# Layer 1's projections of the first sequence as seven block products

## The chip, the cores and the metric

The kernel runs on one core of a Trainium2 chip. The time is the device time of one execution in microseconds (us). TensorE is the matrix engine (PE in the rows; PEld is its weight loads), VectorE is DVE, ScalarE is ACT, GpSimd is POOL, and SP is the engine whose queue issues the DMAs. Each engine runs its own instructions in order and waits on semaphores for the others.

## The reference

Two sequences, p of 1024 tokens and s of 512, with 1024 channels, go through the same two layers. All is in float32.

```python
def trunk(x, ...):
    for layer in range(2):
        mix = even_mixer(x, ...) if layer % 2 == 0 else odd_mixer(x, ...)
        x = layer_norm(ALPHA * x + mix, ln_g[layer], ln_b[layer])

def odd_mixer(x, w_in, q_norm_g, k_norm_g, w_out):          # layer 1
    proj = x @ w_in                                          # [T,1024] @ [1024,2560]
    q, k, v, z = jnp.split(proj, IN1_SPLIT_POINTS, axis=-1)  # 1024, 256, 256, 1024
    q = rms_norm(q.reshape(B, T, 8, 128), q_norm_g)
    k = rms_norm(k.reshape(B, T, 2, 128), k_norm_g)
    q, k = apply_axial_rope(q, cos, sin), apply_axial_rope(k, cos, sin)
    o = blocked_attention(q, k, v)                           # 8 query heads, 2 of k and v
    return (o * jax.nn.silu(z)) @ w_out
```

`even_mixer` (layer 0) is a pooling mixer and a bidirectional mLSTM behind one input projection; the change leaves its work as it is.

## The kernel before, in words

Every matrix product is made of three: each float32 operand is split into a rounded high half and the rest, and `mm` is called for high by high, high by low and low by high. A weight unit is 128 channels by 512 columns (256 KB). `wunit` loads it through SP, GpSimd makes its high half (`hi_pool`), VectorE the low one (`lo_dve`). `mm` is line L97 for every product, so groups are told apart by the names of their tiles.

The stages follow one another:

1. Layer 0's first stage, to about 173 us: the projection of both sequences by weights `wt`. The x blocks (`xrp`, `xrs`) are loaded and split in its first piece.
2. The heads of layer 0, to about 600 us.
3. The mid stage, to about 759 us: layer 0's output projection (`o0p`, `o0s`) by tiles of 128 tokens, its layer norm, the store of the result to `x1` in DRAM, and, a tile or two later, eight transposes of the tile (`x1t`), whose split halves (`XH`, `XL`) stay in SBUF for layer 1. `mid_tiles` lists the tiles, p's eight and then s's four. The last head's transposes (`hTs`) lie among its first tiles.
4. kv of layer 1 (`layer1_kv`, 759 to 831 us): eight weight units, twelve tiles of 128 tokens. `tok_proj` gives a tile of 512 columns, k and v; v is split, k goes through `rope` and a transpose.
5. q (`layer1_qz`, 831 to 975 us): two pieces of 512 columns, each eight units, for twelve tiles. `rope` does the norm's sum of squares on ACT, the power on GpSimd (L929), the products with the tables on VectorE (L931, L936) and their sum on GpSimd (L937); four transposes (`Tq`), an ACT copy and a store to DRAM follow.
6. z (`z_block`, 975 to 1104 us): eight blocks of 128 columns by 1024 channels for three groups of 512 tokens, with silu on ACT and a store. The first unit's scores (`Sp`) are woven into the last blocks.
7. Attention and the output projection, to the end.

The order of the instructions of an engine is the order in which the program's scheduler puts them by its own model of costs, from the order of the code. It is fixed when the program is built. Tiles are taken from rings with a set number of buffers (`bufs`), and PSUM banks too (`mm` 2, `me` 3, `mx` 1, `mc` 2): an instruction that writes one waits for the last reader of the tile before.

Of the kernel before, what the change touches and what calls it, by code (L numbers as in the profile page):

```python
# [56 lines left out]
class Kern:  # L57
    def __init__(self, ctx, tc, a):
# [5 lines left out]
        self.z0, self.xcd = {}, {}  # L64
        self.wlight = False
# [188 lines left out]
    def layer0(self, seqs):  # L254
# [4 lines left out]
        with ExitStack() as ctx:  # L259
# [4 lines left out]
            with ExitStack() as c1:  # L264
# [6 lines left out]
                self.wbufs, self.rbufs = 10, 4  # L271
                self.gate_places(gp)
# [620 lines left out]
    def mid_spread(self, t, y):  # L893

        _, _, gi, i = self.mid_tiles[t]
        c = slice(i * P, (i + 1) * P)
        for half in range(2):
            pt = self.bank("mc", f"x1t{gi}{i}{half}")
            for j in range(4):
                k = 4 * half + j  # L900
                self.nc.tensor.transpose(pt[:, j * P:(j + 1) * P], y[:, k * P:(k + 1) * P], self.idn)
            for j in range(2):
                xh, xl = (x[gi][2 * half + j][:, :, c] for x in (self.XH, self.XL))
                pv = pt[:, 256 * j:256 * j + 256].rearrange("p (k t) -> p k t", t=P)
                self.hi_act(xh, pv)
                self.lo_dve(xl, pv, xh)
# [12 lines left out]
    def rope(self, ps, nh, n, tabs, t1, t2, name):
# [11 lines left out]
        nc.vector.tensor_tensor(out=t1[:, 0:W].rearrange("p (h f) -> p h f", f=P), in0=ps.rearrange("p (h f) -> p h f", f=P),  # L931
# [8 lines left out]
    def rope_consts(self, which, g, tiles):  # L940
        nc = self.nc
        self.load(g.rearrange("p a f -> p (a f)"), self.a["g4"][256 * which:256 * which + 256].partition_broadcast(P))
        for i, n in enumerate(("cos", "sin")):
            t = tiles[i]
            self.load(t, self.a[n])
            nc.vector.tensor_tensor(out=t, in0=t, in1=g[:, i:i + 1, :].to_broadcast([P, 8, P]), op=ALU.mult)
# [13 lines left out]
    def layer1_kv(self):  # L960

        nc, a, hp = self.nc, self.a, self.hp
        tags = iter([f"x{p}{k}{h}" for h in (1, 0) for k in range(KD) for p in "lh"])
        place = lambda name, shape=(P, 512): self.x0p.tile(list(shape), F32R, tag=next(tags), name=name)
        self.Kh, self.Kl, self.Vh, self.Vl, self.rq = {}, {}, {}, {}, {}
        for s in self.seqs:
            T = self.seqs[s][0]
            self.Kh[s], self.Kl[s] = ([[place(f"K{x}{s}{kv}{c}") for c in range(T // 512)] for kv in range(2)] for x in "hl")
            self.Vh[s], self.Vl[s] = ([place(f"V{x}{s}{c}", (P, 2, 256)) for c in range(T // 256)] for x in "hl")
            self.rq[s] = self.cp.tile([P, T // P, 8], F32, name=f"rq{s}")  # L970
        self.spare = list(tags)
# [12 lines left out]
        g = self.raw("rg1", (P, 2, P))
        tabs = self.rope_consts(1, g, [hp.tile([P, 8, P], F32, tag=("w", "pl")[i], name=f"rt1{i}") for i in range(2)])
        for gi, (s, g) in enumerate(self.groups):
            for i in range(4):
# [360 lines left out]
```

## Time and profile before

| | us |
|---|---|
| median of three runs | 1557.92 |
| the three runs | 1551.84, 1557.92, 1557.95 |
| profiled execution | 1552.2 |
| its span | 1550.5 |
| TensorE's mean granted clock | 0.979 of full speed |

Three kinds of views are used below. The windows give, for a stretch of time, each engine's busy time with its count of instructions, TensorE's granted clock, the DMA engines' share and GB/s. The chain of work that ended last is followed back from the last instruction, each step to what released it. Rows of instructions give the start, the length, the line and the operation (out<-in); matmuls overlap, so their pace is read from one start to the next. A group's row has the busy time and the mean length in ns.

### The profile page before, as it was taken

What the parts mean: (1) busy time and instruction counts of PE and PEld (TensorE: products, weight loads), DVE (VectorE), ACT (ScalarE), POOL (GpSimd) and SP (SyncE); (2) the same over time, 40 slices, a digit from 0 to 9 for tenths busy, and PEclk for the clock granted to TensorE, in tenths of its full rate; (3) what the DMA queues carried; (4) which work ended last, traced back from release to release, by engine and by line L of the source; (5) the groups of instructions that cost most, each with busy time, mean ns of one, the idle gap of its engine ahead of it and who ended that gap; (6) DMA issues with size and microseconds to landing.
All of it is one profiled execution on the core that took longest, in us unless ns stands there. A gap on an engine that the chain in (4) does not pass through costs nothing.

```text
span 1550.5 us, 20820 instructions
## 1 busy us (share of the span) xinstructions
PE 1489.5 (96%) x7166; PEld 1221.7 (79%) x7166; DVE 921.7 (59%) x1894; ACT 666.3 (43%) x1522; POOL 630.8 (41%) x652
## 2 busy tenths in 40 slices
PE   8999998999997899999999999999989999999997
PEld 7877787878876778777778888888778888888886
DVE  5242265586867888847754452311377777777775
ACT  4122354455545665334221332213565555555651
POOL 3101234343464654535433454301244444454642
PEclk9999999999998899999999999999999999999999
DMA  7302342234434556444502131321241111111211
GB/s 229 122 30 69 95 123 95 96 103 129 144 122 150 179 168 198 150 141 152 172 7 88 59 102 55 122 89 69 66 138 28 55 55 55 55 55 55 82 62 55
DMA packets 125305, 155.77 MB, mean 100 GB/s; under 512 B 9472, under 2 KB 71424, under 8 KB 125200
## 3 DMA queue, kind: packets, MB, share of 16 engines
q1 hardware_dynamic: 125200, 154.45, 31.3%
q8 instruction: 56, 0.92, 0.2%
q14 instruction: 49, 0.40, 0.1%
HBM read 107.18 MB, written 47.24 MB: 100 GB/s over the span
## 4 chain that ended last, share of the span: by engine, by line
PE 62%; DVE 15%; DMA 10%; issue 5%; ACT 4%; POOL 3%; SPq 0%; DVEq 0%; ACTq 0%; POOLq 0%
PE q L97 9%; PE z L97 8%; PE Sp L97 6%; PE Op L97 6%; PE o1p L97 5%; PE ptp L1134 4%; PE kv L97 3%; PE o1s L97 3%; PE tp L97 3%; PE zp L97 2%; PE ts L97 2%; PE zs L97 2%; PE Ss L97 1%; PE Os L97 1%; DMA wo0r<-wo 1%
## 5 line engine op out<-in xcount | busy, mean ns | idle before, releaser
L1112 POOL TENSOR_SCALAR prp<-prp,smp 128x1024 f32<-128x1024 f32 x64 | 72.7, 1136 | 137.6 <-DVE smp L1111 131.3
L87 ACT CAST pwp<-ptp 128x512 fp32r<-128x512 f32 x128 | 74.8, 584 | 95.0 <-PE ptp L1134 94.7
L97 PE MATMUL Op<-pwp,Vhp 128*128 128x512 f32 x256 | 109.0, 426 | 1.4 <-DVE pwp L90 1.4
L90 DVE TENSOR_TENSOR pwp<-ptp,pwp 128x512 fp32r<-128x512 f32 x128 | 87.3, 682 | 29.1 <-ACT pwp L87 29.1
L1107 ACT ACTIVATE prp<-Sp,nbp,rqp 128x1024 f32<-128x1024 f32 (+1 forms) x68 | 78.7, 1158 | 27.1 <-DVE nbp L1104 20.7
L1099 DVE TENSOR_REDUCE nbp<-Sp 128x1 f32<-128x1024 f32 (+1 forms) x68 | 78.2, 1153 | 15.7 <-PE Sp L97 15.6
L1134 PEld LDWEIGHTS ptp<-idn,prp 128*128 128x128 f32 x512 | 63.7, 140 | 21.5 <-POOL prp L1112 2.2
L1134 PE MATMUL ptp<-idn,prp 128*128 128x128 f32 x512 | 77.1, 272 | 3.4 <-POOL prp L1112 1.8
L97 PE MATMUL z<-x1h,wz_h 128*128 128x512 f32 x192 | 76.0, 396 | 0.0
L97 PE MATMUL z<-x1l,wz_h 128*128 128x512 f32 x192 | 75.7, 394 | 0.0
L97 PE MATMUL z<-x1h,wz_l 128*128 128x512 f32 x192 | 75.6, 395 | 0.0
L97 PE MATMUL q<-wq_h,x1l 128*128 128x512 f32 x144 | 57.2, 398 | 0.0
L97 PE MATMUL q<-wq_l,x1h 128*128 128x512 f32 x144 | 56.8, 396 | 0.0
L97 PE MATMUL q<-wq_h,x1h 128*128 128x512 f32 x144 | 56.3, 400 | 0.0
L97 PEld LDWEIGHTS Op<-pwp,Vhp 128*128 128x128 f32 x256 | 48.3, 189 | 8.8 <-DVE pwp L90 1.9
L97 PE MATMUL tp<-wt_h,xhp 128*128 128x512 f32 x128 | 51.1, 409 | 2.8 <-ACT wqk_r L248 2.8
L97 PE MATMUL o0p<-wo0h,ah0p 128*128 128x512 f32 x128 | 50.5, 400 | 1.9 <-DVE xr0p L835 1.9
L97 PE MATMUL o0p<-wo0l,ah0p 128*128 128x512 f32 x128 | 50.6, 396 | 0.7 <-POOL wo0l L94 0.7
L97 PE MATMUL tp<-wt_h,xlp 128*128 128x512 f32 x128 | 51.0, 404 | 0.0
L97 PE MATMUL tp<-wt_l,xhp 128*128 128x512 f32 x128 | 50.9, 402 | 0.0
L97 PE MATMUL o0p<-wo0h,al0p 128*128 128x512 f32 x128 | 50.7, 397 | 0.0
L97 PE MATMUL Op<-pwp,Vlp 128*128 128x512 f32 x128 | 50.1, 391 | 0.0
(804 smaller groups left out, 4691.9 us busy)
## 6 DMA issues: line engine op xcount, KB each, us to landing
wt_r<-w0t SPq DMA_DIRECT2D x16, 256.0 KB, 4.5
xrp<-xT_p SPq DMA_DIRECT2D x16, 256.0 KB, 3.6
xrs<-xT_s SPq DMA_DIRECT2D x16, 256.0 KB, 3.2
wp<-rd_p SPq DMA_DIRECT2D x16, 256.0 KB, 5.0
z_p<-zsp SPq DMA_DIRECT2D x16, 256.0 KB, 3.4
szp<-z_p SPq DMA_DIRECT2D x16, 256.0 KB, 3.0
wo0r<-wo SPq DMA_DIRECT2D x16, 256.0 KB, 4.4
ar0p<-act_p SPq DMA_DIRECT2D x16, 256.0 KB, 2.9
```

The source lines that it names most:

```text
L87: self.nc.scalar.copy(out, in_)
L90: self.nc.vector.tensor_tensor(out=out, in0=in_, in1=hi.bitcast(F32), op=ALU.subtract)
L97: self.nc.tensor.matmul(out, lhsT=lhsT, rhs=rhs, start=start, stop=stop)
L1099: nc.vector.tensor_reduce(out=nb[:, i:i + 1], in_=b, op=ALU.max, axis=AX.X, negate=True)
L1107: nc.scalar.activation(pr[:, i * W:(i + 1) * W], b, AF.Exp, bias=nb[:, 0:1], scale=rq, accum_out=sm[:, i:i + 1])
L1112: nc.gpsimd.tensor_scalar(pr, pr, sm, 0.0, ALU.mult, ALU.add)
L1134: nc.tensor.transpose(pt[:, h * P:(h + 1) * P], prs[h][:, c * P:(c + 1) * P], self.idn)
```

## The change

For p alone, kv, z and q of layer 1 are taken by the scheme of Strassen and Winograd. The tokens are two halves and the channels two halves, so x is four blocks A11, A12, A21, A22; the weight of a q piece pair, of a z block pair or of kv (k and v columns) is four blocks as well. In place of eight block products there are seven, P1 to P7, four of them with a sum of x blocks or a sum of weight blocks on a side, or both. Their results are added into the four output blocks.

```diff
+    PRODUCTS = (("P1", "A11", (0, 0)), ("P2", "A12", (1, 0)), ("P6", "S2", 1), ("P5", "S1", 0),
+                ("P3", "S4", (1, 1)), ("P7", "S3", 2), ("P4", "A22", 3))
```

A number in the last place is a sum of weights, a pair is a plain block.

- `weight_sums`, in layer 0's first stage: ten sets (kv 2, q 4, z 4). A set is four loads of 256 KB, four subtractions (two on GpSimd, two on VectorE) and four stores to DRAM. Two sets are begun behind each of five groups of that stage.

```diff
+                for o, e, x, y, d in ((0, nc.gpsimd, (0, 1), (0, 0), (0, 0)), (2, nc.vector, (1, 1), (0, 1), (0, 1)),
+                                      (1, nc.gpsimd, (1, 1), (0, 0), (1, 1)), (3, nc.vector, (1, 1), (1, 0), (1, 0))):
+                    e.tensor_tensor(out=r[d], in0=r[x], in1=r[y], op=ALU.subtract)
+                    self.load(self.sums[kind][k, o], r[d])
...
+                        if piece or gi:
+                            for _ in range(2):
+                                next(presums, None)
```

- `mid_pair`, in the mid stage: tiles of p are taken in pairs, one of each half, and the list of tiles is reordered to 0, 4, 1, 5, 2, 6, 3, 7. Behind the transposes come the halves of A11, A12, A22 and, by adds on VectorE, of S1, S2 and S3 (high half on ACT, low half on GpSimd). S4 = A12 - S2 is made in kv, behind P2 (`last_sum`), on VectorE and GpSimd by turns.

```diff
+    K.mid_tiles = [("p", 4 * g + i, g, i) for i in range(4) for g in range(2)] + [("s", i, 2, i) for i in range(4)]
...
+        s1 = f("s1", ("y0", "sza")[i % 2])
+        nc.vector.tensor_tensor(out=s1, in0=a21, in1=p22, op=ALU.add)
...
+        nc.vector.tensor_tensor(out=s2, in0=s1, in1=p11, op=ALU.subtract)
+        nc.vector.scalar_tensor_tensor(out=a21, in0=a21, scalar=-1.0, in1=p11, op0=ALU.mult, op1=ALU.add)
```

- The products. kv's have 256 columns and are done first, then z (`z_pair`, four pairs of blocks), then q. For each product and tile `gathered` adds the result on VectorE (P1 is an ACT copy) to the running sums `u` and, where an output block is complete, to a tile `c`; P7 needs two such adds.

```diff
+                for k in range(4):
+                    ah, al = self.a_part(b, k)
+                    wh, wl = (w[:, k % nk * W:(k % nk + 1) * W] for w in cur[k // nk])
+                    self.mm(ps, ah[:, c], wh, k == 0, False)
+                    self.mm(ps, ah[:, c], wl, False, False)
+                    self.mm(ps, al[:, c], wh, False, k == 3)
+                self.gathered(prod, i, ps, u, W, finish, f"{name}{i}")
...
+        if prod in done:
+            o, a = done[prod]
+            c = a if prod in ("P7", "P4") else self.tp.tile([P, 512], F32, tag="c", name=f"c{name}{o}", bufs=2)[:, 0:W]
+            add(c, a, ALU.subtract if prod == "P4" else ALU.add)
+        if prod == "P1":
+            nc.scalar.copy(u2, ps)
+        elif prod in ("P6", "P7"):
+            add(u2, u2)
+        elif prod == "P5":
+            add(u4, u2)
+        if prod in done:
+            finish(o, i, c)
```

- For p the high halves of weights are made on ACT (`prepare`), and rope's first product on GpSimd instead of VectorE (`mul`).

```diff
-        nc.vector.tensor_tensor(out=t1[:, 0:W].rearrange("p (h f) -> p h f", f=P), in0=ps.rearrange("p (h f) -> p h f", f=P),
+        mul.tensor_tensor(out=t1[:, 0:W].rearrange("p (h f) -> p h f", f=P), in0=ps.rearrange("p (h f) -> p h f", f=P),
                                 in1=ct[:, n:n + 1, :].to_broadcast([P, nh, P]), op=ALU.mult)
```

- s comes behind p: its x1 is read back from DRAM and transposed there, and kv, q and z are done for it as before, with the weights loaded and split a second time. The first scores are woven into z's blocks of s.

```diff
+            y = self.x1p.tile([P, D], F32, tag=f"x1{'hl'[i % 2]}0{i // 2}", name=f"y1{i}")
+            self.load(y, self.x1[s][i])
...
+        units = [self.wunit(a["w1kv"][k], f"wkv{k}") for k in range(KD)]
```

In counts: matmuls of 512 columns for p go from 384 to 336 in q and in z; in kv 192 of 512 columns become 336 of 256. Weight units loaded for p go from 40, shared with s, to 70, and s loads 40 of its own.

Three places show how the instructions now stand.

First VectorE in kv of p. Before, in the middle of kv (`Vlp` and `Klp` are low halves of v and k, `kr` a k row, `ssk` its sum of squares, L931 and L936 rope's products, L999 the scaling):

```order
L90 TENSOR_TENSOR Vlp1_7510<-kv03_7719,Vhp1_7506 128x256
L90 TENSOR_TENSOR Klp10_7503<-kT01_7663,Khp10_7499 128x128
L999 TENSOR_SCALAR kr02_7699<-kr02_7699,rsk02_7704 128x128 x2
L927 TENSOR_SCALAR ssk03_7747<-ssk03_7747 128x2
L931 TENSOR_TENSOR kr03_7746<-kv03_7719,rt10_7571 128x256
L936 TENSOR_TENSOR kr03_7746<-kv03_7719,rt11_7572 128x128 x2
L999 TENSOR_SCALAR kr03_7746<-kr03_7746,rsk03_7751 128x128 x2
L90 TENSOR_TENSOR Vlp2_7511<-kv10_7766,Vhp2_7507 128x256
L90 TENSOR_TENSOR Klp00_7501<-kT02_7710,Khp00_7497 128x128
```

After, where P6 and P5 end (`u` the running sums, `ckv` a finished block, L975 to L977 and `S4l` the sum S4, `wlkv` the low half of a weight unit, `rt` rope's tables, L1006 rope's second product):

```order
L977 TENSOR_TENSOR s4a0_7953<-s4a0_7953,s4b0_7954 128x512
L1016 TENSOR_TENSOR rt1kp_7731<-rt1kp_7731,rgkp_7729 128x1024
L1094 TENSOR_TENSOR u11_7726<-u01_7722,kvP5i1_8075 128x256
L91 TENSOR_TENSOR wlkv06_7794<-kv011_r_7795,whkv06_7793 128x512
L91 TENSOR_TENSOR S4l0_7949<-s4a0_7953,S4h0_7945 128x512
L1006 TENSOR_TENSOR kr110_7820<-ckv011_7818,rt1kp_7731 128x128 x2
L1006 TENSOR_TENSOR kr111_7855<-ckv111_7853,rt1kp_7731 128x128 x2
L91 TENSOR_TENSOR wlkv17_7800<-kv111_r_7801,whkv17_7799 128x512
L975 TENSOR_TENSOR s4a2_7967<-A12h1_6724,A12l1_6726 128x512
L1094 TENSOR_TENSOR ckv211_7888<-u02_7723,kvP2i2_7875 128x256
L1094 TENSOR_TENSOR ckv311_7923<-u03_7724,kvP2i3_7910 128x256
L976 TENSOR_TENSOR s4b2_7968<-S2h1_6728,S2l1_6730 128x512
```

The k rows of one tile, which stood together, are parted by S4's sums, the tables, weight units and the adds that free TensorE's banks.

Second GpSimd at the end of q of p. Before, in the middle of q (`tq` is a q row, `wq1` a weight unit of the second piece):

```order
L937 TENSOR_TENSOR tq021_8672<-tq021_8672 128x512
L84 TENSOR_SCALAR wq14_h_8820<-wq14_r_8818 128x512
L84 TENSOR_SCALAR wq15_h_8826<-wq15_r_8824 128x512
L84 TENSOR_SCALAR wq16_h_8832<-wq16_r_8830 128x512
L84 TENSOR_SCALAR wq17_h_8838<-wq17_r_8836 128x512
L929 TENSOR_TENSOR rsq022_8728<-ssq022_8722,mhalf_83 128x4
L937 TENSOR_TENSOR tq022_8721<-tq022_8721 128x512
L929 TENSOR_TENSOR rsq023_8777<-ssq023_8771,mhalf_83 128x4
L937 TENSOR_TENSOR tq023_8770<-tq023_8770 128x512
```

After, at P4, where p ends and s begins (`t0qp` is a q row of p, L1001 rope's first product, L999 the power, L1007 the sum, `wkv` the kv weight units of s):

```order
L85 TENSOR_SCALAR wkv1_h_10096<-wkv1_r_10094 128x512
L85 TENSOR_SCALAR wkv2_h_10102<-wkv2_r_10100 128x512
L999 TENSOR_TENSOR rsqp123_9625<-ssqp123_9619,mhalf_86 128x4
L1007 TENSOR_TENSOR t0qp123_9617<-t0qp123_9617,t1qp123_9618 128x512
L85 TENSOR_SCALAR wkv3_h_10108<-wkv3_r_10106 128x512
L999 TENSOR_TENSOR rsqp220_9688<-ssqp220_9682,mhalf_86 128x4
L1001 TENSOR_TENSOR t0qp220_9680<-u10_7725,rt0qp_8426 128x512
L999 TENSOR_TENSOR rsqp221_9727<-ssqp221_9721,mhalf_86 128x4
L1007 TENSOR_TENSOR t0qp220_9680<-t0qp220_9680,t1qp220_9681 128x512
L1001 TENSOR_TENSOR t0qp221_9719<-u11_7726,rt0qp_8426 128x512
L85 TENSOR_SCALAR wkv4_h_10114<-wkv4_r_10112 128x512
L85 TENSOR_SCALAR wkv5_h_10120<-wkv5_r_10118 128x512
```

A row has three operations in place of two, and the units that s's kv tiles need stand among p's last four rows.

Third SP in layer 0's first stage, around the last x block of the first group. Before:

```order
L81 DMA wqT_r_355<-wqT 128x512
L81 DMA wkT_r_361<-wkT 128x512
L81 DMA xrp70_307<-xT_p 128x512
L81 DMA xrp01_397<-xT_p 128x512
L81 DMA xrp11_415<-xT_p 128x512
L81 DMA xrp21_433<-xT_p 128x512
L81 DMA xrp31_451<-xT_p 128x512
```

After (`srkv` are the loads for the sums, `sum_kv` the stores of them):

```order
L82 DMA xrp01_400<-xT_p 128x512
L82 DMA srkv010_560<-w1kv 128x2x256
L82 DMA srkv100_570<-w1kv 128x2x256
L82 DMA srkv101_572<-w1kv 128x2x256
L82 DMA srkv111_574<-w1kv 128x2x256
L82 DMA xrp11_418<-xT_p 128x512
L82 DMA srkv110_576<-w1kv 128x2x256
L82 DMA xrp21_436<-xT_p 128x512
L82 DMA sum_kv_57<-srkv000_554 128x512
L82 DMA sum_kv_57<-srkv001_556 128x512
L82 DMA xrp31_454<-xT_p 128x512
L82 DMA sum_kv_57<-srkv011_558 128x512
```

The x blocks `xrp01` to `xrp31` of p's second group, which stood next to each other, have loads for the sums between them, and `xrp31` stands behind two stores that wait for the subtractions.

More of the change, by code (lines that the diff above doesn't have):

```diff
@@ L64, in __init__ @@
         self.z0, self.xcd = {}, {}
+        self.sums = {n: d.tile([k, 4, P, 512], F32, name=f"sum_{n}") for n, k in (("kv", 2), ("q", 4), ("z", 4))}
         self.wlight = False
@@ L891, in mid_tile, with turned @@
         self.pend.append((t, xr))
-    def mid_spread(self, t, y):
-        _, _, gi, i = self.mid_tiles[t]
-        c = slice(i * P, (i + 1) * P)
[L897 to L906, printed above, removed]
+    def turned(self, y, half, tag, name):
+        pt = self.bank(tag, name)
+        for j in range(4):
+            k = 4 * half + j
+            self.nc.tensor.transpose(pt[:, j * P:(j + 1) * P], y[:, k * P:(k + 1) * P], self.idn)
+        return pt
@@ L921, in rope, with a_part @@
+    def a_part(self, b, k):
+        if b == "S4":
+            return tuple(x[k] for x in self.S4)
+        return tuple(x[k // 2][:, k % 2, :] for x in self.A[b])
+    def rope(self, ps, nh, n, tabs, t1, t2, name, mul):
         nc = self.nc
@@ new lines, in next_units, with gathered @@
+    def next_units(self, n):
+        while len(self.ready) < self.wbufs:
+            u = next(self.coming, None)
+            if u is None:
+                break
+            self.prepare(u, *(self.wp.tile([P, 512], F32R, tag=t, name=f"{t}{u[0]}{u[1]}{len(self.ready)}", bufs=self.wbufs) for t in ("wh", "wl")))
+        out, self.ready = self.ready[:n], self.ready[n:]
+        return out
+    def gathered(self, prod, i, ps, u, W, finish, name):
+        nc = self.nc
+        u2, u4 = (x[i][:, 0:W] for x in u)
+        add = lambda out, a, op=ALU.add: nc.vector.tensor_tensor(out=out, in0=a, in1=ps, op=op)
+        done = {"P2": ("11", u2), "P3": ("12", u4), "P7": ("22", u4), "P4": ("21", u2)}
+        if prod in done:
[10 more added lines that the diff above has]
+            finish(o, i, c)
@@ new lines, in token_products @@
+    def token_products(self, name, nk, W, u, finish, after=None):
+        for j, (prod, b, _) in enumerate(self.PRODUCTS):
+            cur = self.next_units(4 // nk)
+            for i in range(4):
+                ps = self.bank(("mm", "me")[i % 2], f"{name}{prod}i{i}")[:, 0:W]
+                c = slice(i * P, (i + 1) * P)
+                for k in range(4):
+                    ah, al = self.a_part(b, k)
[4 more added lines that the diff above has]
+                self.gathered(prod, i, ps, u, W, finish, f"{name}{i}")
+            if after and j == 1:
+                after()
@@ new lines, in layer1_in, with kv_done @@
+        table = lambda which, names, nt=8: self.rope_consts(which, tp.tile([P, 2, P], F32, tag="rg", name=f"rg{names}"),
+                                                            [tp.tile([P, nt, P], F32, tag=f"rt{i}", name=f"rt{i}{names}") for i in range(2)], nt)
+        tabs = table(1, "kp")
+        group = {"1": 0, "2": 1}
+        def kv_done(o, i, c):
+            g = group[o[0]]
+            if o[1] == "1":
+                self.k_rows(p, g, i, c, tabs, tp.tile([P, 2, 256], F32, tag="t", name=f"kr{o}{i}", bufs=4), self.nc.gpsimd)
+            else:
+                self.v_rows(p, 4 * g + i, c)
@@ L1238, in layer1 @@
                         weights(1, range(KD))
[L1239 removed]
+                        ts = [tp.tile([P, 512], F32, tag="c", name=f"ln1{j}", bufs=2) for j in range(2)]
                         ts += [self.raw(f"ln1{j}") for j in range(2, 4)]
```

297 lines of the change are left out of this document (198 added, 99 removed).

## The prediction

> **What bounds the kernel now.** I read the page's busy times first, then a table of the projection stage and its neighbours by windows, the chain of work that ended last inside that stage, TensorE's waits just before it, and single rows for prices.
>
> Busy times of the page, then the windows (us, us of each engine with its count, granted clock, DMA share, GB/s):
>
> ```profile
> PE 1489.5 (96%) x7166; PEld 1221.7 (79%) x7166; DVE 921.7 (59%) x1894; ACT 666.3 (43%) x1522; POOL 630.8 (41%) x652
> ...
> 0.00:173.00 173.00, 165.80 (x716) 131.86 (x717) 61.70 (x85) 46.26 (x76) 28.96 (x51) 0.96 0.32 107
> ...
> 600.00:759.00 159.00, 149.89 (x711) 122.76 (x710) 115.37 (x283) 62.44 (x135) 80.37 (x71) 0.99 0.52 166
> 759.00:831.00 72.00, 71.47 (x326) 57.60 (x326) 39.27 (x123) 18.67 (x84) 22.43 (x31) 1.00 0.11 35
> 831.00:975.00 144.00, 144.00 (x669) 117.26 (x669) 64.54 (x189) 40.76 (x218) 70.01 (x65) 1.00 0.28 84
> 975.00:1104.00 129.00, 129.00 (x560) 104.11 (x558) 22.95 (x45) 33.47 (x57) 18.96 (x24) 1.00 0.28 92
> ```
>
> TensorE is busy 96% of the span. Layer 1's kv (759 to 831), q (to 975) and z (to 1104) leave it idle for half a microsecond in 345 us at full clock, and the next busiest engine reaches 55% of a stage (VectorE in kv). So the chain there is matmul after matmul (start, length, count):
>
> ```profile
> 804.56 5.57 PE kv L97 x24
> ...
> 984.48 58.80 PE z L97 x253
> ```
>
> 58.80/253 = 0.2324 us for each matmul of 512 columns. What is taken off here is time, unless something new makes TensorE wait.
>
> **The products.** A product over one block of p (512 tokens by 512 channels in, 512 columns out) is four tiles of 12 matmuls. q and z: eight block products each became seven: 2 x 384 matmuls become 2 x 336, 96 fewer: 96 x 0.2324 = 22.3 us. kv: 192 matmuls of 512 columns become 336 of 256. The trace has none of 256, but neighbours:
>
> ```profile
> 297.06 0.27 PE L97 MATMUL Ap<-vhp,plp 128*128 128x130 f32 x1
> 297.17 0.34 PE L97 MATMUL Up<-vwhp,ktp 128*128 128x260 f32 x1
> ...
> 297.47 0.40 PE L97 MATMUL Up<-vwhp,ktp 128*128 128x260 f32 x2
> 297.71 0.28 PE L97 MATMUL Up<-vwlp,ktp 128*128 128x260 f32 x1
> 297.83 0.28 PE L97 MATMUL Up<-vwhp,ktp 128*128 128x260 f32 x1
> 297.95 0.39 PE L97 MATMUL xbp<-xhp,xbp2u_h 128*128 128x512 f32 x1
> ```
>
> 260 columns start 0.12 us apart (130 columns 0.11), each with a weight load of its own. 336 x 0.12 = 40.3 against 192 x 0.2324 = 44.6: 4.3 less. Together **-26.6 us**. The transposes are as many as before.
>
> A weight load lasts longer than that pace:
>
> ```profile
> L97 PEld LDWEIGHTS z<-x1h,wz_h 128*128 128x128 f32 x192 | 36.1, 188 | 8.3
> ```
>
> The Trainium skill, Perfetto Trace Analysis, section Identifying the Most-Contended Engine, tells one to judge TensorE by the summed time of weight loads rather than by matmul time. The rows above speak against adding these up: loads of 0.188 us passed at a pace of 0.12, so they overlap. By the page's measure the halved columns of kv would gain nothing; that is a rival below.
>
> **kv: VectorE becomes as full as TensorE.** Prices:
>
> ```profile
> 797.70 0.42 DVE L931 TENSOR_TENSOR kr<-kv,rt 128x256 f32<-128x256 f32 x1
> 798.03 0.48 DVE L936 TENSOR_TENSOR kr<-kv,rt 128x128 f32<-128x128 f32 x2
> 799.11 0.29 DVE L90 TENSOR_TENSOR Klp<-kT,Khp 128x128 fp32r<-128x128 f32 x1 [0.59 <-ACT Khp L87]
> 799.46 0.48 DVE L999 TENSOR_SCALAR kr<-kr,rsk 128x128 f32<-128x128 f32 x2
> ...
> 766.42 2.36 DVE L946 TENSOR_TENSOR rt<-rt,rg 128x1024 f32<-128x1024 f32 x2 [0.35 <-DMA rg<-g]
> ...
> L90 DVE TENSOR_TENSOR wz_l<-wz_r,wz_h x16: 679/693/1772, 971.5 to 1043.8; 128x512 fp32r<-128x512 f32 x16
> ...
> 899.21 1.25 DVE L1032 TENSOR_SCALAR rqs<-rsq 128x4 f32<-128x4 f32 x1 [0.78 <-POOL rsq L929]
> ...
> 899.14 1.30 POOL L937 TENSOR_TENSOR tq<-tq 128x512 f32<-128x512 f32 x1
> ```
>
> From 797.70 to 798.03 a 256-column operation costs 0.33. After: 28 gathering adds x 0.33 = 9.2; low halves of about 14 weight units x 0.69 = 9.7; S4's two quarters on VectorE, three operations each, and four low halves, 10 x 0.69 = 6.9; tables 2.4; eight k rows at 0.48 + 0.48 + 4 x 0.29/2 (they start about 0.2 apart) = 1.5 each, 12; eight v rows 2.6. That is 42.8 us, against TensorE's 40.3 plus 16 transposes. Nothing is hidden comfortably: the first tile of P5 needs a bank that P2's add must free, and P3 waits for S4, whose sums stand among the k rows. The last two rows show what may come on top: an operation of 128x4 took 1.25 us and ended with the GpSimd operation beside it. GpSimd now runs beside VectorE in kv (k rows' products, powers and sums, S4's other quarters). Lowest 0 (perfect interleaving); highest +11 (VectorE's total plus 8 us, if its twenty subtractions and sums with both inputs in SBUF stretch by 0.4). I take **+6**, z's start included: between the ends, since what VectorE has over at the end of kv falls into z, which needs it little.
>
> The Trainium skill, SBUF — State Buffer, section SBUF: two separate sides, calls the port pair that VectorE and GpSimd share an exclusive lock: a VectorE operation with two SBUF inputs, or in a two-port mode, waits for the whole GpSimd operation. The trace agrees with the 1.25 beside 1.30. By that rule every such operation of kv may meet a GpSimd one, the kv term is the +11, and the sum 5 higher.
>
> **z** brings 28 units in 78 us: 0.69 + 0.5 us of VectorE (low half, one 512 add of at most 0.69) per 2.8 us of TensorE. Nothing waits. The 70 units of p and the 40 read again for s are 70 loads of 256 KB more, 18 MB over 320 us, 57 GB/s beside rows of 84 to 92 at a share of 0.28: hidden. The first scores, taken among z's last blocks before and among s's blocks now, are the same matmuls.
>
> **End of q of p: GpSimd.** Rope's first product for p moves to it:
>
> ```profile
> 907.85 1.30 POOL L937 TENSOR_TENSOR tq<-tq 128x512 f32<-128x512 f32 x1 [0.39 <-DVE ssq L927]
> 909.10 1.01 POOL L929 TENSOR_TENSOR rsq<-ssq,mhalf 128x4 f32<-128x4 f32 x1
> 910.09 1.29 POOL L937 TENSOR_TENSOR tq<-tq 128x512 f32<-128x512 f32 x1
> ...
> 904.87 0.62 POOL L84 TENSOR_SCALAR wq_h<-wq_r 128x512 fp32r<-128x512 f32 x1 [2.24 <-DMA wq_r<-w1q]
> ```
>
> A row of q now costs 1.25 + 1.0 + 1.25 = 3.5 us there. P3, P7 and P4 finish four rows each: 42 us in 3 x 48 x 0.2324 = 33.5, the first one ready 2.8 late: GpSimd is 11.3 behind when q's matmuls end. Then eight high halves of s's kv weights (5.0) stand among its rows, and TensorE's next work for s needs them. Cover: s's 32 transposes (3.6) and a kv tile of 5.6 between two rows. Lowest 0, highest 11.3 + 5.0 - 3.6 = 12.7. I take **+6**, the middle: the order puts tiles of s between the waiting transposes, but VectorE, blocked now and then as above, hands the rows over late. The cover gone, it is the high end.
>
> **First stage: 40 loads and 40 stores on SP.**
>
> ```profile
> 15.07 0.33 SPq L81 DMA_DIRECT2D wkT_r<-wkT  x1
> 15.68 12.93 SPq L81 DMA_DIRECT2D xrp<-xT_p  x9
> ...
> 15.00:57.00 42.00, 39.22 (x168) 31.49 (x167) 20.74 (x33) 15.61 (x27) 6.71 (x11) 0.96 0.61 201
> ...
> wt_r<-w0t SPq DMA_DIRECT2D x16, 256.0 KB, 4.5
> ...
> PE tp L97 <- ACT wqk_r L248: 2.8, 1, 2.8
> ```
>
> 21 MB at the window's rate for a full share (201/0.61 = 330 GB/s) are 64 us of DMA in a stage with 0.32 of 173 taken: room on average, not at the start. The last x block of p's second group was issued at 28.6; now 16 loads and 8 stores, 6.3 MB or 19 us, are queued ahead of it on SP: 47.6, landing 3.6 to 4.5 later near 52. That group of 96 matmuls (22.3 us) ends at 57 now, the 2.8 us wait in it; its eighth step begins at 57 - 2.8 = 54, or at 51 if that wait shrinks. So up to +1 there, and +2 for s's blocks, which stand behind stores that wait for subtractions: **+3**, from -1 (the 2.8 us wait for wqk_r shifts into it) to +12 (two starts that late and the clock falling with them).
>
> **Mid (600 to 759).** TensorE's waits, and the clock after the longest:
>
> ```profile
> PE hTs L715 <- ACT ths L714: 4.7, 2, 3.9
> PE o0p L97 <- DVE xr0p L835: 1.9, 1, 1.9
> PE x1t L901 <- DVE x1l L90: 1.8, 2, 1.4
> ...
> 683.00:687.00 4.00, 3.65 (x11) 2.80 (x12) 1.98 (x3) 1.96 (x5) 0.00 (x0) 0.57 0.54 197
> ```
>
> The tiles' new order leaves the hTs chain where it was (a load, VectorE, GpSimd, ACT), with about twelve matmuls fewer ahead of it: up to +3. The wait for x1l can go (s is transposed later, from x1 read back), and the making of S1 to S3 hides (24 subtractions of 256 columns at half of 1.25, 15 us of GpSimd beside 80 of 159; ACT has 62): **-1**, from -5 (waits and slow clock gone) to +4.
>
> **Sum.** -26.6 + 6 + 6 + 3 - 1 = -12.6 on the profiled execution's 1552.2: 1539.6. The median of the three runs (1557.92) stands 5.7 above that execution, which agrees with their fastest; I carry under half of it: **1542**.
>
> **Rivals.**
> 1. The waits all reach their high ends (kv +11, q +12.7, first stage +3, mid 0): -26.6 + 26.7 = 0, with the same carry about 1555. For: VectorE's sum above TensorE's in kv. Against: z's slack, where lateness is absorbed.
> 2. Weight loads set kv's pace: 336 x 0.188 = 63.2 instead of 40.3, VectorE then covered: 1542 + 23 - 5 = 1560. Against: the 0.12 pace.
> 3. Slower: SP, in order, stops behind stores. A set's four subtractions alternate between GpSimd and VectorE (2 x 1.30 + 2 x 0.69 = 4.0 after 4.5 of landing); a step of two sets is 12.5. If two steps are not covered, the x and weight blocks behind them come 25 us late and the clock falls: 1542 + 25 = 1567. It decides from a first stage that ends 20 us later than 173. Against: loads of a step stand well ahead of its stores.
> 4. The waits do not appear (kv, q and first stage 0, mid -4): -30.6, 1524.
> That the products are not fewer is excluded by the order of TensorE's instructions.
>
> **Chances.** The sum 0.60 (its own range 1529 to 1553), rival 1 0.18, rival 2 0.05, rival 3 0.10, rival 4 0.07. Half a per cent, 7.8 us, is about what a measurement of this kernel can tell from no change: faster means below 1550.1. Faster: 0.56 of the sum, 0.07 of rival 4, 0.03 of rival 1, together 0.66. Within: 0.04, 0.13 of rival 1, 0.04 of rival 2, 0.02 of rival 3, 0.23. Slower: 0.02 of rival 1, 0.01 of rival 2, 0.08 of rival 3, 0.11. The range, 1523 to 1559, leaves out rival 3, half of rival 2 and some of rivals 1 and 4.
>
> **What would show it.** The chain in q and z of p should still read 0.232 us per matmul, with 336 each; kv's 256-column matmuls 0.12 apart, not 0.19. TensorE's waits should name VectorE (u, S4) in kv for about 6 us, GpSimd's rope rows or high halves after q of p for about 6, and little in z. GpSimd should be busy without a gap in the last 45 us of q of p. The first stage should end 2 to 4 us later. The forecast fails if the clock falls in a stage where it was 1.00, if VectorE's kv work runs well past z's start, or if SP's queue holds x blocks back.

## The result, and the profile after

| | before | after |
|---|---|---|
| median, six runs each (us) | 1557.16 | 1572.66 |
| span of the profiled execution | 1550.5 | 1563.2 |
| mean granted clock | 0.979 | 0.974 |
| ratio, 95% interval | | 1.0104 [1.0076, 1.0133] |

The kernel is 1% slower. 1542 with a range to 1559 was forecast; the rivals that end on the slower side (weight loads that set kv's pace, SP's queue in the first stage) aren't what happened either. The medians differ by 15.5 us, the profiled executions, each among the fastest of its kernel, by 12.7. The starts of the stages tell where these 12.7 lie:

| stretch (us) | before | after | difference |
|---|---|---|---|
| first stage, to the heads' first matmul | 173.7 | 171.3 | -2.4 |
| heads, to the first tile of the mid stage | 425.1 | 427.4 | +2.3 |
| mid, to layer 1's first matmul | 160.1 | 153.4 | -6.7 |
| layer 1's projections, to the first attention transpose | 346.0 | 367.5 | +21.5 |
| the rest | 445.7 | 443.7 | -2.0 |

Of the 6.7 in the mid stage 1.8 are 16 of s's transposes, which only moved; before, the other 16 stood in kv. Layer 1's 367.5 are kv of p 57.4, z 80.4, q 86.5 and s 143.2. The part called s holds s's transposes, kv, q, six of its eight z blocks, the first scores and the transposes of p's last eight q rows: 456 matmuls of 512 columns, 106.0 us at 0.2324, and 104 transposes, 11.4 us at 0.11. That is 117.4, or 113.9 without the 32 transposes of p, so 25.8 of the 143.2 are waits and slow matmuls. The windows, the same columns as in the prediction:

```profile
746.00:802.00 56.00, 43.81 (x298) 40.04 (x297) 46.40 (x85) 17.56 (x49) 35.62 (x31) 0.94 0.39 124
802.00:883.00 81.00, 81.00 (x391) 67.26 (x390) 52.68 (x108) 36.68 (x79) 9.85 (x12) 1.00 0.55 162
883.00:966.00 83.00, 81.81 (x368) 66.15 (x367) 53.52 (x94) 33.46 (x109) 29.96 (x25) 1.00 0.44 137
966.00:1118.00 152.00, 135.94 (x592) 106.28 (x590) 104.95 (x233) 57.76 (x213) 96.23 (x97) 0.93 0.45 132
```

Z and q of p are nearly as dense as before, at full clock. The first and the last row are not: TensorE is idle for 12 and 16 us there, and its clock falls. In kv the VectorE column is above TensorE's. Slices of 5 us show both it and the clock, and TensorE's waits name it:

```profile
775.00:780.00 5.00, 2.85 (x12) 2.55 (x12) 5.00 (x8) 0.95 (x2) 4.22 (x4) 0.66 0.14 26
780.00:785.00 5.00, 3.53 (x18) 3.53 (x19) 5.00 (x9) 1.91 (x9) 5.00 (x5) 0.70 0.01 2
785.00:790.00 5.00, 3.64 (x26) 3.09 (x25) 5.00 (x11) 1.15 (x3) 3.68 (x5) 0.96 0.00 0
790.00:795.00 5.00, 4.31 (x33) 3.70 (x32) 5.00 (x15) 1.43 (x5) 3.11 (x3) 1.00 0.38 105
```

```profile
PE kvP5i L98 <- DVE ckv L1094: 3.6, 1, 3.6
PE kvP7i L98 <- DVE ckv L1094: 2.2, 1, 2.2
PE kvP5i L98 <- DVE u L1094: 1.8, 1, 1.8
```

VectorE has no gap for 20 us; TensorE waits for the adds that free its banks. VectorE's rows of that time, with GpSimd's beside them (start, length):

```profile
775.71 1.76 DVE L91 TENSOR_TENSOR S4l<-s4a,S4h 128x512 fp32r<-128x512 f32 x1
777.40 1.96 DVE L1006 TENSOR_TENSOR kr<-ckv,rt1kp 128x128 f32<-128x128 f32 x4
...
781.67 1.10 DVE L976 TENSOR_TENSOR s4b<-S2h,S2l 128x512 f32<-128x512 f32 x1
782.70 1.44 DVE L1137 TENSOR_SCALAR kr<-kr,rskp 128x128 f32<-128x128 f32 x2
```

```profile
775.20 1.73 POOL L975 TENSOR_TENSOR s4a<-A12h,A12l 128x512 f32<-128x512 f32 x1
776.89 1.72 POOL L976 TENSOR_TENSOR s4b<-S2h,S2l 128x512 f32<-128x512 f32 x1
...
780.50 1.72 POOL L977 TENSOR_TENSOR s4a<-s4a,s4b 128x512 f32<-128x512 f32 x1
782.19 1.17 POOL L1007 TENSOR_TENSOR kr<-kr 128x256 f32<-128x256 f32 x1
```

S4l takes 1.76 where 0.68 is the least for that shape; two scalings of 128 columns take 1.44 where they took 0.48; GpSimd's sums of 512 columns take 1.72 where 1.29 was the row of before. Both engines stretch. S4l starts 0.5 us into the GpSimd row of 775.20 and ends 0.5 behind that row's end.

Behind q of p both engines are nearly full:

```profile
966.00:976.00 10.00, 8.01 (x30) 6.05 (x29) 9.67 (x24) 1.87 (x9) 8.32 (x8) 0.83 0.46 137
976.00:986.00 10.00, 5.18 (x23) 3.14 (x22) 10.00 (x18) 4.16 (x20) 9.52 (x11) 0.87 0.42 125
986.00:996.00 10.00, 9.10 (x40) 7.31 (x41) 5.50 (x16) 4.54 (x23) 5.82 (x5) 0.79 0.22 61
```

TensorE's waits of that part (the longest for VectorE, and GpSimd's) name VectorE more than GpSimd: 10.3 us in all for VectorE from 968 to 1120, 3.6 for ScalarE, 3.4 for GpSimd.

```profile
PE kvs L98 <- DVE x1l L91: 2.8, 3, 1.7
PE x1t L903 <- DVE x1l L91: 2.1, 2, 2.0
PE qP4i L98 <- DVE u L1094: 2.0, 1, 2.0
PE Tqp L1159 <- POOL t0qp L1007: 1.4, 1, 1.4
```

In q itself GpSimd was not full: in the last 45 us of q's matmuls it was busy for 22.9. The chain shows one reason. The finished blocks `c` have two places, a q row is stored from its place, and so the third and fourth row of P2, and of P3, start only when the stores of the first two have landed (store, VectorE's add, rope):

```profile
916.10 4.25 DMA qd_p<-cq
920.44 0.70 DVE cq L1094
...
952.69 4.09 DMA qd_p<-cq
956.87 0.70 DVE cq L1094
```

GpSimd stands idle for 7.4 and 7.2 us in front of these two pairs of rows, and the work that it lacks there falls behind q.

The products themselves came as costed. P2 of kv passes at 0.12 us a matmul, and the 84 matmuls of each z pair take 19.5 us, 0.232 each:

```profile
760.20 0.28 PE L98 MATMUL kvP2i<-kv3h,A12h 128*128 128x256 f32 x1
760.32 0.28 PE L98 MATMUL kvP2i<-kv3l,A12h 128*128 128x256 f32 x1
760.43 0.28 PE L98 MATMUL kvP2i<-kv3h,A12l 128*128 128x256 f32 x1
...
850.86 19.53 PE z4P L98 x84
```

### The profile page after: what moved, and what is told of

It reads as the page before. It is cut to its first block, busy times and chain, and to the rows that moved or that the text cites. A ratio compares the mean times of both kernels' runs of the same rounds, so it can differ in the third digit from the quotient of the medians.

```text
span 1563.2 us, 21698 instructions
## 1 busy us (share of the span) xinstructions
PE 1474.5 (94%) x7214; PEld 1211.3 (77%) x7214; DVE 1077.7 (69%) x2062; ACT 722.2 (46%) x1628; POOL 727.9 (47%) x726
## 4 chain that ended last, share of the span: by engine, by line
PE 59%; DVE 20%; DMA 9%; ACT 4%; issue 4%; POOL 2%; SPq 1%; DVEq 0%; ACTq 0%; POOLq 0%
PE Sp L98 6%; PE Op L98 5%; PE o1p L98 5%; PE tp L98 4%; PE ptp L1357 3%; PE o1s L98 3%; PE o0p L98 3%; PE zp L98 3%; PE qs L98 3%; PE ts L98 2%; PE z L98 2%; DVE t1qp L1006 1%; PE o0s L98 1%; PE Ss L98 1%; PE z4P L98 1%
## 5 line engine op out<-in xcount | busy, mean ns | idle before, releaser
L1001 POOL TENSOR_TENSOR t0qp<-cq,rt0qp 128x512 f32<-128x512 f32 x8 | 10.7, 1339 | 107.9 <-DVE cq L1094 100.5
L98 PEld LDWEIGHTS Op<-pwp,Vhp 128*128 128x128 f32 x256 | 48.3, 189 | 7.0
L658 DVE SCALAR_TENSOR_TENSOR Usp<-Usp,decbp 128x130 f32<-128x130 f32 x48 | 23.7, 495 | 27.7 <-ACT Usp L623 27.2
L98 PE MATMUL Sp<-Khp,qhp 128*128 128x512 f32 x128 | 42.4, 408 | 0.0
L1335 POOL TENSOR_SCALAR prs<-prs,sms 128x512 f32<-128x512 f32 x32 | 24.3, 761 | 36.1 <-DVE sms L1334 23.8
L98 PE MATMUL Sp<-Klp,qhp 128*128 128x512 f32 x128 | 41.0, 396 | 0.0
L98 PE MATMUL Sp<-Khp,qlp 128*128 128x512 f32 x128 | 40.8, 395 | 0.0
```

The source lines that it names most:

```text
L98: self.nc.tensor.matmul(out, lhsT=lhsT, rhs=rhs, start=start, stop=stop)
L658: nc.vector.scalar_tensor_tensor(out=U[:, i, :], in0=U[:, i + o, :], scalar=dec[:, 4 * d + h, n:n + 1], in1=U[:, i, :], op0=ALU.mult, op1= ...
L1001: mul.tensor_tensor(out=t1[:, 0:W].rearrange("p (h f) -> p h f", f=P), in0=ps.rearrange("p (h f) -> p h f", f=P), in1=ct[:, n:n + 1, :].to ...
L1335: nc.gpsimd.tensor_scalar(pr, pr, sm, 0.0, ALU.mult, ALU.add)
```

## The experiments

Each kernel is the changed one with the edit shown. Single profiles are compared by the lengths of stages: what lies ahead of layer 1 ends up to 8 us apart from run to run (the mid stage starts between 596 and 604), and the totals with it. Stages that an edit leaves alone differ too: kv of p took 56.9 to 59.5 us and s 139 to 146 in such runs.

**Rope's first product of p on VectorE**

```diff
-    ... tp.tile([P, 2, 256], F32, tag="t", name=f"kr{o}{i}", bufs=4), self.nc.gpsimd)
+    ... tp.tile([P, 2, 256], F32, tag="t", name=f"kr{o}{i}", bufs=4), self.nc.vector)
-    self.q_rows(p, ..., tabs, f"qp{o}{i}", self.nc.gpsimd, t1, t2, c)
+    self.q_rows(p, ..., tabs, f"qp{o}{i}", self.nc.vector, t1, t2, c)
```

> Rope's first product for p goes back from GpSimd to VectorE (kv and q). In the changed kernel kv of p lasted 57.4 us (42 without waits), z 80.2, q of p 86.5 and s's part 143 (about 119 without waits). Theory 1, GpSimd is the bound behind q of p and its operations and VectorE's stretch each other: GpSimd loses 1.25 us of 3.5 per q row and VectorE gets 0.6; s's part gets at least 8 us shorter and kv at least 4. Theory 2, VectorE's amount of work is the bound: kv gets 8 x 0.33 = 3 us longer and q of p longer too. Theory 3, kv starts late behind the mid stage's last tile and s waits for tables and weight loads: neither changes by over 3 us.

1551.5 us in one run, kv 56.2, q of p 82.7, s 135.8. Theory 1 for q and s: 3.8 and 7.4 less (s just short of the 8 expected), GpSimd's work in s 81 instead of 96 us. For kv it isn't: 1.2. Behind q TensorE waits for GpSimd's rows and for VectorE's:

```profile
PE Tqp L1159 <- POOL t0qp L1007: 5.3, 4, 2.5
PE kvs L98 <- DVE x1l L91: 4.1, 3, 2.2
```

**z of p ahead of kv**

```diff
-        order = [("kv", k, b) ...] + [("z", k, b) ...]
+        order = [("z", k, b) ...] + [("kv", k, b) ...]
+            if b == 0 and j == 1:
+                self.last_sum()
```

> For p the order is z, kv, q instead of kv, z, q; S4 is made in z's first pair. kv and z of p together lasted 137.6 us. Theory 3 (kv's adds stand on VectorE behind the layer norm of the last tile of the mid stage and wait for that tile's store, then everything is late): z covers this and the tables, and the two together come to 125 us or less, kv's own waits under 5. Theories 1 and 2 (stretching, or too much work on VectorE): kv keeps at least 8 of its 15 us of waits wherever it stands, 132 or more together.

130.8 us for both instead of 137.8, z 89.9 and kv 40.9. Neither theory's number, and each half right: kv keeps no wait, as theory 3 said, and the total is near that of the others. The kv row (second) has no idle TensorE, 31 of 41 us on VectorE; z in front (first) has the waits and the clock instead:

```profile
756.00:806.00 50.00, 45.34 (x167) 34.45 (x166) 35.54 (x52) 18.98 (x31) 20.44 (x14) 0.86 0.60 189
...
846.00:887.00 41.00, 41.00 (x343) 40.87 (x342) 30.99 (x81) 18.28 (x58) 11.66 (x15) 1.00 0.35 104
```

So kv's own work on VectorE is hidden under seven products of 256 columns. It isn't hidden together with S4, the tables' first load, and the mid stage's last norms and units. GpSimd's work went from its side as well (11.7 us in this row, 35.6 in kv of the changed kernel), so the run doesn't part the two engines.

**Tables of s in places free before**

```diff
-        tabs = ... tp.tile([P, 8, P], F32, tag=f"rt{i}", name=f"rts{i}")
+        tabs = ... self.x1p.tile([P, 8, P], F32, tag=f"x1h0{2 + i}", name=f"rts{i}")
```

> Rope's tables for s lie in places that are free before q of p ends, instead of in a pool that opens when p's closes. s's part lasted 143 us; its tables were issued at 1009 to 1013 and the first k row of s began at 1025.8, 50 us after s's first matmul. If the late tables are what holds s back: 135 or less. If it is GpSimd's rows of p (theory 1) or the weight loads that stand behind q's stores on SP: within 3 us of 143.

s 136.7, q of p 88.6. Less by 6.5, 1.7 short of the number for "the tables hold s back"; 2 came back in q. A part of the cause at most.

**No weight sums**

```diff
-                                next(presums, None)
-            self.load(raw, self.sums[kind][k, b])
+            self.load(raw..., self.piece(kind, k, b // 2, b % 2))
```

> The weight sums are left out (no loads, subtractions and stores in layer 0's first stage), and the products read plain weight blocks of the same size in their place. The first stage ended 4 us earlier than in the kernel before, against +3 in the prediction. If the sums are hidden: first stage and total within 2 us of the changed kernel. If the earlier end came from them (the wait of 2.9 us for wqk_r went because the order changed): the wait comes back and the stage is 2 to 4 us longer. If they still cost: shorter by 2 us or more.

The heads begin at 170.8 instead of 171.3, layer 1 at 750.0 instead of 752.0. (In the kernel before the heads began at 173.7, so the stage had become 2.4 us shorter, not 4.) TensorE's wait for wqk_r comes back in part (1.7 us), those for VectorE's gate rows shrink from 3.0 and 1.5 to 0.8 and 0.7, and the stage is no longer for it: the earlier end did not come from that wait. The 80 DMAs cost half a microsecond in their stage and at most 2 up to layer 1. The single run took 1558.2 us, 6.9 less than the profiled execution of the changed kernel; 4 of them lie in s, which took 139.1 with the same instructions. So much a stage of one run differs from another's.

**Places of their own for kv's first units; c laid out first; high halves of s on ACT; all together**

```diff
+        raw = self.raw(f"{nm}_r") if own is None else self.x0p.tile([P, 512], F32, tag=own, name=f"{nm}_r")
```

> The first eight weight units of kv are loaded into eight places of their own instead of a ring of two. In the changed kernel VectorE's low halves of units 5 to 7 wait for these loads (2.0 us and 1.4 us idle), the last tile's layer norm stands behind them, and the first add of P2 starts 15.4 us after P1. Theory 3a, the late loads in a ring of two: kv 57.4 falls to 52 or less and the first add comes within 11 us of P1. Theory 3b, the place of the last tile that P2's tile c takes over (its store ended 2.2 us before the add): within 2 us of 57.4, since the norm and the store are what they were.

kv 56.0, the first add 12.9 us after P1 (14.8 in the changed kernel, 766.76 against 752.00; the 15.4 of the expectations mixes two starting points), and P1 itself 3 us later: the loads had moved behind a store of the mid stage in SP's order. Theory 3a falls.

```diff
+        for i in range(2):
+            tp.tile([P, 512], F32, tag="c", name=f"cpad{i}", bufs=2)
```

> In the pool of kv and q of p the ring of c is laid out first, so that c takes the place of a tile that is stored earlier than the mid stage's last one. Theory 3b (the adds wait for the store of the last tile): the first add comes 2 to 5 us earlier and kv falls from 57.4 to 54 or less. Theory 3a, or VectorE's own rows ahead of the adds: kv within 2 us of 57.4.

The wait for the store shrank from 2.17 to 0.23 us, the first add came 2.2 us earlier against P1, and kv was 56.9 instead of the 54 or less of theory 3b. The wait was real and cost nothing.

```diff
+        elif getattr(self, "sact", False):
+            self.hi_act(wh, raw)
+            self.lo_dve(wl, raw, wh)
```

> The high halves of the weights of s (40 units) are made on ACT instead of GpSimd, 0.6 us each. GpSimd's rows after q of p lose 8 x 0.62 = 5 us of other work. If GpSimd's backlog of q rows holds s up: s's part, 143 us, falls by 5 or more. If VectorE and the stores on SP hold it: by less than 3.

`sact` is set for the units of s. s 134.2 us: 9 less, and 5 under the lowest of the runs that leave s alone. GpSimd's load is a cause.

> The four edits together with rope's first product of p on VectorE: own places for kv's first units, c laid out first, tables of s in free places, high halves of s on ACT. If the waits add up as theory 1 (q and s) and theory 3 (kv) say: kv 50 or less, q of p 83, s 130 or less, the total 1540 or less. If the gains cover the same waits: about 1550, as the product on VectorE alone gave.

1553.76 us against 1553.15, ratio 1.0006 [0.9983, 1.0029]: kv 54.1, q 83.8, s 134.1. The bounds named for a gain were missed. Three edits that each took 6 to 9 us off s take 9 together, as if they acted on one wait.

**s's z blocks first; twelve units ahead; both**

```diff
+        self.token_products("q", 1, 512, u, q_done, {2: lambda: s_tiles((0, 1)), 3: lambda: s_tiles((2, 3))})
...
+        for b in range(6):
```

> Rope's first product on VectorE, tables of s in free places, high halves of s on ACT, and another order for s: its transposes behind P6 and P5 of q of p, then its z blocks (which need no rope), then kv and q of s. The chain of s from the end of q of p lasted 143 us in the changed kernel and 134 with these edits but not the order. If TensorE waits there because GpSimd's and VectorE's rows of p lie in front of s's kv (in-order engines, no work of TensorE's to cover them): z covers 33 us of them and s takes 125 or less. If s's own rows or weight loads are the bound: 131 or more. kv of p, not touched, stays at 55 to 58.

134.6 us for s, no better, and q of p, which now holds s's first transposes, took 90.1. TensorE waited 12 us for rows of GpSimd's (5.9 in one) with z's matmuls behind them in its order.

> z before kv for p, as before, with twelve instead of eight weight units made ahead in places that are free at that time. z first gave 130.8 us for both, kv 40.9 and z 89.9 (78 without waits). VectorE, 42 us of work in kv and begun 15 us late, was the length of kv there; in z it has slack. If z's 12 us of waits came from units that could not be loaded before the last tile of the mid stage left its place: z 83 or less, both together 124 or less. If from S4 or the low clock: 88 or more.

z 91.1 and both together 132.1: the units weren't it. TensorE's longest wait in z was 4.5 us for an add of VectorE's.

> The last two together. If the waits are two independent ones, at the handing over from the mid stage and behind q of p, the times add: 12 us or more below the product on VectorE alone (1551), 1540 or less, faster than the kernel before by 0.8% or more. If they are one (GpSimd and VectorE simply full): 1548 to 1552.

1560.11 us, ratio 1.0040 [1.0018, 1.0062], slower than both forecasts. Both remedies as they stood were wrong.

**Transposes written later, alone and with c first; the last norm left out**

```diff
+        if late is not None:
+            late.append((s, n, piece, out, out, nm))
```

> As the kernel with s's z blocks first, but the transposes of q's last eight rows of p (from P7 and P4) are written in the code four rows later, the last four among s's z blocks. There TensorE waited 12 us for rows of GpSimd's (one wait of 5.9) with z's matmuls ready behind them, and s lasted 134.6 us. If TensorE's order is what turns GpSimd's lateness into waits: those waits fall to 4 or less and s to 126 or less. If GpSimd and VectorE are full through s: 132 or more, the waits elsewhere.

s 134.7. But the waits that the edit was to remove stayed: 11.6 us for q's rows, instead of 12. So it doesn't decide whether TensorE's order is a cause. The slices speak against the order alone: VectorE had no gap, and GpSimd hardly one.

```profile
976.00:986.00 10.00, 6.12 (x32) 4.53 (x30) 10.00 (x25) 4.33 (x21) 9.59 (x6) 1.00 0.27 79
986.00:996.00 10.00, 3.67 (x14) 2.47 (x15) 10.00 (x25) 6.00 (x26) 9.01 (x6) 0.50 0.74 210
```

Z's matmuls need all four tiles of s split, which VectorE does too; the last of s's transposes started at 993.9, 0.5 us after such a wait, and z's first matmul at 996.5.

> The same with c laid out first in its pool (which let P2's add start 2 us sooner). If both are causes: 1545 or less, faster than the kernel before by 0.5% or more. If TensorE's order was not the cause: 1555 to 1570, as the kernel with s's z blocks first.

1564.13 us, ratio 1.0075 [1.0044, 1.0106], in the range named for "not the cause".

```diff
+        if name == "0s3":
+            self.load(dst, xr)
+            return
```

> As the changed kernel, but the layer norm of the mid stage's last tile (of s) is left out, its sum is stored as it is. In the changed kernel VectorE's first add of kv started 15.4 us after TensorE's first matmul, behind this norm (3.5 us of VectorE, 1 of GpSimd and the waits between) and its store; VectorE then worked 42 us without a pause worth naming, and kv lasted 57.4. If kv's length is that late start plus VectorE's amount of work: the first add comes 4 to 6 us earlier and kv is 51 to 54. If kv's waits come from the stretching beside GpSimd or from loads: kv stays within 2 us of 57.4.

The first add came 10.1 us after P1 instead of 14.8 (757.83 against 747.71), and kv took 58.6. The late start is not the cause. TensorE waits where it did, and for the same:

```profile
PE kvP5i L98 <- DVE ckv L1097: 4.8, 1, 4.8
PE kvP7i L98 <- DVE ckv L1097: 2.9, 1, 2.9
PE kvP5i L98 <- DVE u L1097: 1.8, 1, 1.8
```

**q between z's pairs**

```diff
+        order += [("z", k, b) for k in range(2) ...] + [("q", k, b) ...] + [("z", k, b) for k in (2, 3) ...]
```

> The order for p is kv, two of z's four pairs, q, the other two pairs, and then s as in the changed kernel. Nothing else is changed. Behind q of p VectorE and GpSimd were busy 10.0 and 9.6 us of 10 while TensorE waited (two thirds idle, at half clock), and s lasted 143 us against some 119 of its matmuls. Z needs no GpSimd and a third of VectorE. If the backlog of q's rows is the cause, 39 us of z cover it: s (from the end of p's products to the first attention transposes) falls to 130 or less, the z behind q stays under 45. If s is slow by itself (its second loads and splits): 140 or more. kv: as it was, 55 to 58.

s 122.1 us, 21 less, and 8 above the 113.9 of its own matmuls and transposes (the 119 of the expectations was too high): the backlog of q's rows held s for most of its waits. The two pairs of z behind q took 53.5 instead of 39, over the 45 expected. q's last transposes stand among their matmuls, and TensorE waits 8.0 us there for GpSimd's q rows. kv, at 59.5, was over its bound too. In the three rows (q, z, s) the idle time of TensorE has moved into the middle one, and shrunk; 14 of the 21 us came back there. Z in front of s also gives the loads and splits of s more time, which the run doesn't part from the backlog:

```profile
855.00:941.00 86.00, 82.55 (x373) 66.31 (x372) 59.10 (x110) 37.18 (x128) 36.75 (x28) 1.00 0.35 106
941.00:995.00 54.00, 46.03 (x200) 35.94 (x200) 39.77 (x71) 21.29 (x66) 31.85 (x28) 0.94 0.64 198
995.00:1117.00 122.00, 116.84 (x529) 93.55 (x528) 71.12 (x169) 46.35 (x148) 60.12 (x67) 0.99 0.42 128
```

> The same with the high halves of s on ACT and rope's first product of p on VectorE. If backlog and GpSimd's work in s are both causes: s 125 or less, the total 1543 or less, faster than the kernel before by 0.5% or more. If the edits act on one and the same wait: about what the better of them gives, 1550.

1550.72 against 1553.79 us, ratio 0.9973 [0.9953, 0.9993]: p's last pairs 50 us, s 124.3. The first version that is faster than the kernel before, and by less than forecast: about the 1550 of the other case, in which the edits take the same wait.

> The kernel with z split, ACT for s and rope on VectorE, and two more edits: the first two z pairs go ahead of kv (S4 is made in the first), and c is laid out first in its pool. kv behind z took 40.9 us, no more than its matmuls, against 56 at the front, while z at the front took 12 us more. If the two remedies (z ahead of kv, z behind q) are independent, 5 to 7 us less than without these edits: 1545 or less, ratio about 0.993. If z's 12 us at the front eat what kv gains: within 3 us of 1551.

1547.34 against 1550.33 us, ratio 0.9976 [0.9960, 0.9991], above the 1545 and 0.993 that were forecast for independent remedies. In its profile kv has its 43.5 us without a gap, and layer 1 takes 350.5 us, 3.5 less than without the last two edits and 17 less than the changed kernel; the ratio does not tell it from the version above. Layer 1's 350.5 are still more than the 346.0 of the kernel before, as in every version tried. What this one gains lies in the mid stage (155.2 against 160.1, 1.8 of it moved transposes) and behind layer 1 (442.2 against 445.7). The matmuls that layer 1 saves have not shortened it in any run. What is left stands in the first row and the last two (z at the front, z behind q, s):

```profile
753.00:801.00 48.00, 43.48 (x158) 33.05 (x157) 33.32 (x49) 17.82 (x29) 19.60 (x14) 0.86 0.60 190
801.00:844.50 43.50, 43.50 (x355) 42.93 (x355) 33.46 (x95) 20.51 (x63) 7.53 (x10) 1.00 0.39 114
...
928.00:976.00 48.00, 42.91 (x196) 33.48 (x196) 35.58 (x74) 24.12 (x73) 20.64 (x14) 1.00 0.60 193
976.00:1103.00 127.00, 118.52 (x529) 95.29 (x528) 64.75 (x169) 64.23 (x181) 36.44 (x34) 0.96 0.43 132
```

## Why the prediction was wrong, step by step

- **The products, -26.6.** Right: 0.12 us a matmul in kv, 0.232 in z and q, 336 each. Rival 2, weight loads setting kv's pace, is out: loads passed at 0.12 there as well. The rule of the Trainium skill that stood beside it, from Perfetto Trace Analysis, section Identifying the Most-Contended Engine, gives no time here; the matmuls' pace does.
- **kv, +6 with z's start.** Mis-sized: kv 57.4 - 42.1 and z 80.4 - 78.1 are 17.6. VectorE's sum of 42.8 was the right alarm. The step that failed is the choice between the ends: "what VectorE has over at the end of kv falls into z". TensorE waits for the adds that free its five banks long before kv's end (10.5 us for VectorE in all), slow matmuls follow some of these waits, and the +11 was not an upper bound, since it had neither the clock nor the mid stage's last norms and low halves in it. The rule of the Trainium skill that stood beside it (SBUF — State Buffer, section SBUF: two separate sides) pointed to that end, and the trace agrees with it in kind: S4l takes 1.76 instead of 0.68 beside a GpSimd row of 1.73 that began before it. That it alone makes the wait is not shown: with 26.6 us of GpSimd's work in kv instead of 29.6 kv was only 1.2 shorter, no more than runs differ by. Shown is that kv runs without waits when S4, the tables' load and the mid stage's rest lie elsewhere; which of these it was is open, apart from the last norm, which it was not.
- **End of q of p, +6, at most 12.7.** This is the term that turned the sign: s took 25.8 us more than its matmuls and transposes, q of p 4.9. A backlog of GpSimd was foreseen, but the step costed one engine, as if it were busy throughout and only too slow. In the last 45 us of q GpSimd was busy for 22.9: its rows came late, through VectorE and through the two places of `c`. Behind q VectorE was full as well (10.0 of 10 us), with rows that wait for GpSimd and stretch beside it, and TensorE's waits name it for 10.3 us against 3.4 for GpSimd. The cover that was named, s's transposes, needs VectorE for its own splits. The cover was gone, and there was no other. Covering it by z (122.1) and relieving GpSimd (135.8 and 134.2 instead of 143.2) show the backlog from both sides. What the two places of `c` cost is not shown: no run gave them more, and the two waits for their stores stand in the best version too.
- **First stage, +3.** It ended 2.4 us earlier, and the heads, which the change leaves alone, gave 2.3 back. The wait for wqk_r went, and the waits for VectorE's gate rows grew from 0.8 and 0.7 to 3.0 and 1.5, so the waits do not explain the 2.4. The same number of matmuls was busy for 163.4 us instead of 166.2; why is open. Rival 3, SP's queue, did not come: without the sums the stage ends half a microsecond earlier.
- **Mid, -1.** -6.7, of which 1.8 is moved transposes; the sum had them in neither stage, so they cancel. The rest is the low end of the range: TensorE's waits fell from 9.1 to 4.1 us. The one for hTs shrank from 4.7 to 3.3, and those for xr0p (1.9) and x1l (1.8) went.
- **Sum.** -26.6 + 17.6 + 4.9 + 25.8 + 1.8 for the transposes, less 1.9 that the kernel before lost in layer 1 itself, is 21.6; the projections took 21.5 more. What lies ahead of them and behind gives 8.8 back.
- **The signs named.** Two of the three signs of failure came: the clock fell in kv from 1.00 to 0.94, and VectorE's k rows ran to 823.5, 14 us into z. GpSimd was not busy without a gap at q's end.
- **Rival 1**, all waits at their high ends, was right about kv's VectorE, with an end too low; for q it too had one engine.

## What to carry to other kernels

Fewer products shorten the time only where the engines that gather them have room in the same stretch: add up VectorE and GpSimd for each stage at the durations that they have beside each other, and take a sum close to TensorE's (here 42.8 against 42.1) for a wait. Work that must follow a product (rope, norms) is better placed ahead of a stretch that needs little of those engines than ahead of one that needs them too; here that moved 14 of 21 us and removed the rest. Look at an engine that is late also for what keeps it idle earlier, such as a ring of places. Several edits that each shorten one stage can take the same wait: three of 6 to 9 us gave 9 together.

## What the runs showed of the hardware

A wait can cost TensorE more than its length. Matmuls of 256 columns at kv's start, with the waits ahead of them:

```profile
775.04 0.50 PE L98 MATMUL kvP5i<-kv6h,S1h 128*128 128x256 f32 x1 [1.84 <-DVE u L1094]
775.34 0.41 PE L98 MATMUL kvP5i<-kv6l,S1h 128*128 128x256 f32 x1
775.55 0.41 PE L98 MATMUL kvP5i<-kv6h,S1l 128*128 128x256 f32 x1
...
781.47 0.39 PE L98 MATMUL kvP5i<-kv6h,S1h 128*128 128x256 f32 x1 [3.59 <-DVE ckv L1094]
781.70 0.28 PE L98 MATMUL kvP5i<-kv6l,S1h 128*128 128x256 f32 x1
```

Behind the wait of 1.84 us they pass every 0.21, not every 0.12, and the granted clock of that slice is 0.66. Behind that of 3.59 the first pass every 0.12, in a slice of 0.70. Behind the wait of 2.2 for kvP7i the slice (800 to 805) has 1.00, so not every wait has this price. Over kv and s (0.94 of 56 us, 0.93 of 152) the missing clock is about 14 us, an estimate, out of the 48.3 that kv, z, q and s took beyond their matmuls.

Small operations of VectorE lengthen beside GpSimd too. The 16 scalings of q's rows of p, 128x4, take 0.16 us at the least, 0.241 on average before and 0.877 now. One of 1.25 ends within 0.02 us of the GpSimd operation beside it:

```profile
L1032 DVE TENSOR_SCALAR rqp<-rsq 128x4 f32<-128x4 f32 x16 | 3.9, 241 | 0.6 <-POOL rsq L929 0.6
L1155 DVE TENSOR_SCALAR rqp<-rsqp 128x4 f32<-128x4 f32 x16 | 14.0, 877 | 3.5 <-POOL rsqp L999 3.5
...
975.13 1.25 DVE L1155 TENSOR_SCALAR rqp<-rsqp 128x4 f32<-128x4 f32 x1 [0.33 <-POOL rsqp L999]
975.07 1.29 POOL L1007 TENSOR_TENSOR t0qp<-t0qp,t1qp 128x512 f32<-128x512 f32 x1
```
